# Buffers of 4 and 8 KB per partition for a fused attention and mixture-of-experts layer on one core

## The chip, the core and the metric

The kernel runs on one core of a Trainium2 chip. The metric is the device time of one execution in microseconds (us). Matrix products run on PE (TensorE); DVE, ACT and POOL (VectorE, ScalarE, GpSimd) do the rest; SP (SyncE) issues most DMAs, which 16 DMA engines carry out. On-chip memory (SBUF) has 128 partitions; a buffer's size is given per partition.

## What is computed

The reference, cut to one layer (512 tokens, width 1024, float32):

```python
h = rmsnorm(x, mix_norm);  z = h @ w_in
x = x + concatenate([pool_mixer(u, ...), dsa_attention(q, k, v, qi, ki, wi)]) @ w_out
h = rmsnorm(x, xattn_norm)
x = x + memory_cross_attention(h, mem, ...)        # 256 memory tokens
h = rmsnorm(x, ffn_norm)
x = x + hierarchical_moe(h, ...)                   # top-1 of 4 groups, top-2 of its 8 experts
# each of the 32 experts: out += (silu(h @ w_gate) * (h @ w_up) * gate) @ w_down
# w_gate, w_up: 1024 x 256; w_down: 256 x 1024; so each expert matrix is 1 MB
```

The sparse attention (`dsa_attention`) keeps the 128 best keys of each query by an indexer score.

## The kernel before

**Three stages.** Until about 280 us the kernel projects, finds the best keys (`topk`), attends and adds the output projection; until about 345 us it does the cross-attention and its projections and the routing (`ffn_in`, `route`, `seats`); from about 365 us it runs the experts (`moe_pass`). Weights of the first two stages are loaded raw and split in two float32r parts, `hi` on ACT (L257) and `lo` on DVE or POOL (L259), and multiplied in three products (`mm3`, L342 to L344). Expert weights are used raw in float32.

**Buffers.** All large tiles live in `Slots` (L61): 42 slots of 4 KB (`NSLOT`), and 8 more (`NSLOT2`) once the work area of the first stages is given up (L1148), 50 in all. `get` takes the slot that has been free longest, `put` hands slots back at the end of the list. `take_out` removes a slot for good: the experts take eight in this way, three for gathered rows, two for the turned rows `xt`, two for the results `y`, one for the selection table (`buffer`, `own`). So 42 slots are left for expert weights.

**Loads.** `Stream` (L93) holds all weight loads as one list. `pump` runs whenever something is put back or needed: it splits what is loaded and issues the next load while more than `reserve` slots are free. `do_load` (L247) issues one DMA of 512 KB on SP for each item (L249). The order of the list is written out by hand; where in the program a load is issued follows from when slots come free. SP carries out its DMAs in order, and each waits until the last reader of its slot is done. An expert matrix is two items, its halves `c` = 0 and 1, each with 4 KB per partition out of 8 KB that lie together in HBM (`add_experts`, L1129 to L1139). The items of a pair come as c = 0 of both experts, then c = 1 of both.

**Experts.** Two experts at a time form a pair (`experts`, L1193; 16 pairs), 64 token places each. For pair i PE multiplies gate (32 matmuls, L1203; c = 0 to 7, at each c both experts), transposes the hidden values of pair i - 1 (L1219), turns the gathered rows of pair i + 1 (L1072), multiplies up (L1203), then down of pair i - 1 (L1230). POOL gathers rows with an indirect DMA (`fetch`, L1059) and scatters results into `out` with an accumulating one (L1235). `fetch(i + 3)` in pair i makes, for each second pair, new index tables (`slot_rows`, L1040: `idx`, six buffers); a new `idx` may be written once the scatter that read the old one has landed.

Of the kernel before, what the change touches and what calls it, by code (L numbers as in the profile page):

```python
# [16 lines left out]
P = 128  # L17
# [18 lines left out]
O_U, O_Q, O_K, O_V, O_QI, O_KI = 0, 512, 1024, 1536, 2048, 2560  # L36
NSLOT = 42
NSLOT2 = 8
NG_BUF = 3
# [21 lines left out]
class Slots:  # L61


    def __init__(self, pool, n):
        self.pools, self.free, self.n, self.where = {}, [], 0, {}
        self.on_put = lambda: None
        self.more(pool, n)

    def more(self, pool, n):
        self.pools.update({s: pool for s in range(len(self.pools), len(self.pools) + n)})  # L70
        self.free += list(self.pools)[-n:]

    def get(self, shape, dt):
        s = self.free.pop(0)
        self.n += 1
        t = self.pools[s].tile(shape, dt, tag=f"s{s}", name=f"s{s}_{self.n}")
        self.where[id(t)] = (s, t)
        return t

    def take_out(self):  # L80
        return self.free.pop(0)

    def again(self, s, shape, dt):
        self.n += 1
        return self.pools[s].tile(shape, dt, tag=f"s{s}", name=f"s{s}_{self.n}")

    def put(self, *tiles):
        for t in tiles:
            self.free.append(self.where.pop(id(t))[0])
        self.on_put()  # L90


class Stream:  # L93
# [28 lines left out]
    def pump(self, need=None):  # L122
        if self.busy:
            return
        self.busy = True
        while True:
            force = need is not None and need not in self.out
            keep = 0 if force else self.reserve
            if self.raw and len(self.S.free) >= 2 + keep or self.raw and self.items[self.n_out][4] == "raw":
                self.out_next()  # L130
            elif (self.n_load < len(self.items) and len(self.S.free) >= 1 + keep
                  and (len(self.raw) < self.raw_max)):
# [59 lines left out]
def kernel(ctx, tc, A, out, dbg=None):  # L192
# [9 lines left out]
    ps_tr = ctx.enter_context(tc.tile_pool(name="ps_tr", bufs=PRM["tr"], space=bass.MemoryType.PSUM))  # L202
    S = Slots(slot_pool, NSLOT)

# [283 lines left out]
    def evac_k(t, ps):  # L488
# [10 lines left out]
        if t % 2 == 0:  # L499
            kT[t // 2] = [S.get([P, 2, 4, P], F32R) for _ in range(2)]  # L500
        WV.defer(PRM['lat'], lambda: split_T(qr, kT[t // 2][0][:, t % 2], kT[t // 2][1][:, t % 2], ("kT", t)))
# [95 lines left out]
    def load_bands():  # L597
        pw["b"] = [S.get([P, 1024], F32R) for _ in range(2)]
# [140 lines left out]
    def memory():  # L739
# [8 lines left out]
        dve.tensor_tensor(gqk, vecs[:, V_QN:V_QN + 1], vecs[:, V_KN:V_KN + 1], op=OP.mult)  # L748
        kmT.extend(S.get([P, MH, MT], F32R) for _ in range(2))
        vm.append(S.get([P, 2, 512], F32))  # L750
# [76 lines left out]
    def transposed(t):  # L827

        hl = [S.get([P, NC, P], F32R) for _ in range(2)]
        for k in range(2):  # L830
# [298 lines left out]
    def add_experts(n):  # L1129
        order = [(i - d, name) for i in range(NPR + 1) for d, name in ((0, "gate"), (0, "up"), (1, "down"))]  # L1130
        for i, name in order:
            for c in range(2) if 0 <= i < NPR else ():
                for k, e in enumerate(pairs[i]):
                    w = A[f"w_{name}"][e]
                    if name == "down":
                        src, shape = w.rearrange("(p k) d -> p k d", k=2)[:, c], [P, D]
                    else:
                        src, shape = w.rearrange("(p k) f -> p k f", k=NC)[:, 4 * c:4 * c + 4], [P, 4, FF]
                    ST.add((n, i, name, k, c), src, shape, eng="raw")  # L1139

# [6 lines left out]
    fin = ctx.enter_context(tc.tile_pool(name="fin", bufs=2, reuse_waits="tile"))  # L1147
    S.more(ctx.enter_context(tc.tile_pool(name="slots2", bufs=1, reuse_waits="tile")), NSLOT2)  # L1148
    ST.pump()
# [43 lines left out]
    def experts(n, i, before):  # L1193
# [4 lines left out]
        for u, name in enumerate(("gate", "up")):  # L1198
            W = {(k, c): ST.take((n, i, name, k, c)) for k in range(2) for c in range(2)}
            for c in range(NC):  # L1200
                for k in range(2):
                    ks = slice(k * CAP, (k + 1) * CAP)
                    pe.matmul(pg[ks, u], xt[:, c, ks], W[k, c // 4][:, c % 4],  # L1203
                              start=(c == 0), stop=(c == NC - 1), skip_group_check=True)
            S.put(*(W[k, c] for c in range(2) for k in range(2)))
            if u == 0:
# [9 lines left out]
    def rest(n, i, hid, idx):  # L1216
# [5 lines left out]
        yield  # L1222
        W = {(k, c): ST.take((n, i, "down", k, c)) for k in range(2) for c in range(2)}
        y = own("y", i % 2, [P, D], F32)
        py = [mm_tile([P, 512]) for _ in range(2)]
        for c in range(2):
            for m in range(2):
                for k in range(2):
                    ks = slice(k * CAP, (k + 1) * CAP)
                    pe.matmul(py[m][ks], hT[:, c, ks], W[k, c][:, m * 512:(m + 1) * 512],  # L1230
                              start=(c == 0), stop=(c == 1), skip_group_check=True)
        act.copy(y[:, :512], py[0])  # L1232
        dve.tensor_copy(y[:, 512:], py[1])  # L1233
        S.put(*(W[k, c] for c in range(2) for k in range(2)))
        pool.indirect_dma_start(out=out, out_offset=bass.IndirectOffsetOnAxis(ap=idx, axis=0),  # L1235
# [122 lines left out]
```

## Time and profile before

| what | value |
|---|---|
| time, median of 3 runs (lowest, highest) | 621.26 us (620.33, 622.89) |
| time of the profiled execution | 623.07 us |
| its span | 621.2 us |
| PE, DVE, ACT, POOL busy | 558.6, 312.9, 191.7, 115.1 us |
| queue of SP: packets, bytes, share of 16 DMA engines | 47024, 134.62 MB, 59.6% |
| expert weight loads | 192 DMAs of 512 KB |

The span is from the first to the last instruction of the profiled execution; a share is of the span. The DMA share is the mean busy share of the 16 DMA engines; it can pass 1 a little, as packets overlap. The granted clock of PE stands as a share of full speed. "A <- B" in a list of waits says that A stood idle until B was done.

### The profile page before, as it was taken

What the parts mean: (1) busy time and instruction counts of PE and PEld (TensorE: products, weight loads), DVE (VectorE), ACT (ScalarE), POOL (GpSimd) and SP (SyncE); (2) the same over time, 40 slices, a digit from 0 to 9 for tenths busy, and PEclk for the clock granted to TensorE, in tenths of its full rate; (3) what the DMA queues carried; (4) which work ended last, traced back from release to release, by engine and by line L of the source; (5) the groups of instructions that cost most, each with busy time, mean ns of one, the idle gap of its engine ahead of it and who ended that gap; (6) DMA issues with size and microseconds to landing.
All of it is one profiled execution on the core that took longest, in us unless ns stands there. A gap on an engine that the chain in (4) does not pass through costs nothing.

```text
span 621.2 us, 9049 instructions
## 1 busy us (share of the span) xinstructions
PE 558.6 (90%) x3408; PEld 395.8 (64%) x3408; DVE 312.9 (50%) x752; ACT 191.7 (31%) x366; POOL 115.1 (19%) x94
## 2 busy tenths in 40 slices
PE   8997989999979999999989589979898979899880
PEld 4776766887767777788878466555555555555430
DVE  4598999998996656544435723222222222022000
ACT  5573534424555567764432110101010100001000
POOL 0323331201363000030001211121212121211111
PEclk9998999999989999999989759979897989899996
DMA  8963021326661201129999849999999999999962
GB/s 291 379 207 103 1 69 68 121 82 190 217 216 41 79 0 35 32 79 324 336 338 365 309 135 344 396 397 391 399 382 386 357 383 360 390 355 372 339 222 32
DMA packets 52833, 147.86 MB, mean 238 GB/s; under 512 B 10288, under 2 KB 11056, under 8 KB 52784
## 3 DMA queue, kind: packets, MB, share of 16 engines
q1 hardware_dynamic: 47024, 134.62, 59.6%
q0 software_dynamic: 4608, 8.40, 5.6%
q10 hardware_dynamic: 1152, 4.19, 1.7%
q8 instruction: 29, 0.48, 0.3%
q14 instruction: 20, 0.16, 0.1%
HBM read 142.99 MB, written 12.58 MB: 250 GB/s over the span
## 4 chain that ended last, share of the span: by engine, by line
PE 65%; DMA 15%; DVE 9%; issue 4%; ACT 3%; POOL 2%; SPq 0%; POOLq 0%; DVEq 0%; ACTq 0%
PE mm L1203 15%; PE mm L342 9%; PE mm L343 9%; PE mm L344 8%; PE mm L1230 8%; DMA out_dram<-s,idx 6%; DMA s<-in_w_up_dram 2%; PE sc L352 2%; PE sc L1072 2%; DMA s<-in_w_down_dram 2%; DMA s<-in_w_in_dram 2%; PE tr L1034 2%; PE tr L919 1%; PE tr L698 1%; PE tr L711 1%
## 5 line engine op out<-in xcount | busy, mean ns | idle before, releaser
L1203 PE MATMUL mm<-s,s 128*64 128x256 f32 x1024 | 135.9, 409 | 5.5 <-ACT sg L1208 3.5
L342 PE MATMUL mm<-s,s 128*128 128x512 f32 (+1 forms) x320 | 132.5, 417 | 0.9 <-ACT s L257 0.7
L343 PE MATMUL mm<-s,s 128*128 128x512 f32 (+1 forms) x320 | 127.6, 399 | 1.2 <-DVE s L259 0.8
L344 PE MATMUL mm<-s,s 128*128 128x512 f32 (+1 forms) x320 | 127.6, 399 | 0.0
L1203 PEld LDWEIGHTS mm<-s,s 128*64 128x64 f32 x1024 | 80.1, 147 | 54.7 <-issue 15.3
L342 PEld LDWEIGHTS mm<-s,s 128*128 128x128 f32 (+1 forms) x320 | 60.6, 190 | 16.7 <-issue 2.8
L343 PEld LDWEIGHTS mm<-s,s 128*128 128x128 f32 (+1 forms) x320 | 60.7, 190 | 14.8 <-DVE s L259 1.7
L344 PEld LDWEIGHTS mm<-s,s 128*128 128x128 f32 (+1 forms) x320 | 60.7, 190 | 13.9 <-issue 0.9
L1230 PE MATMUL mm<-s,hT 128*64 128x512 f32 x256 | 64.7, 604 | 1.2 <-issue 1.2
L1232 ACT COPY s<-mm 128x512 f32<-128x512 f32 x16 | 9.4, 585 | 153.1 <-PE mm L1230 153.1
L259 POOL TENSOR_TENSOR s<-s,s 128x1024 fp32r<-128x1024 f32 x17 | 41.2, 2428 | 74.0 <-ACT s L257 72.7
L1235 POOL DMA_INDIRECT out_dram<-s,idx x16 | 25.4, 1584 | 147.0 <-DVE hT L1221 49.4
L257 ACT CAST s<-s 128x1024 fp32r<-128x1024 f32 (+1 forms) x42 | 42.2, 1018 | 30.2 <-DMA s<-in_xattn_wkv_dram 9.4
L1213 DVE SCALAR_TENSOR_TENSOR sg<-mm,gc,sg 128x256 f32<-128x256 f32 x16 | 7.7, 484 | 66.6 <-PE mm L1203 66.6
L1230 PEld LDWEIGHTS mm<-s,hT 128*64 128x64 f32 x256 | 22.0, 141 | 29.1 <-issue 23.5
L259 DVE TENSOR_TENSOR s<-s,s 128x1024 fp32r<-128x1024 f32 (+1 forms) x25 | 33.2, 1331 | 7.0 <-ACT s L257 5.7
L1233 DVE COPY s<-mm 128x512 f32<-128x512 f32 x16 | 11.1, 692 | 48.3 <-PE mm L1230 48.3
L1208 ACT ACTIVATE sg<-mm,gc 128x256 f32<-128x256 f32 x16 | 7.6, 474 | 77.7 <-PE tr L1219 40.3
L1059 POOL DMA_INDIRECT s<-hd,idx x16 | 16.6, 1038 | 72.9 <-DVE idx L1040 66.4
L587 DVE MAX8 m<-s 128x8 f32<-128x256 f32 (+2 forms) x48 | 26.6, 554 | 0.3
L1073 DVE TENSOR_TENSOR s<-sc,gcol 128x1024 f32<-128x1024 f32 x16 | 19.6, 1222 | 13.1 <-PE sc L1072 13.1
L588 DVE MATCH_REPLACE8 s<-m,s 128x256 f32<-128x256 f32 (+2 forms) x48 | 26.0, 541 | 0.0
(209 smaller groups left out, 697.7 us busy)
## 6 DMA issues: line engine op xcount, KB each, us to landing
s<-in_w_up_dram SPq DMA_DIRECT2D x64, 512.0 KB, 11.4
s<-in_w_gate_dram SPq DMA_DIRECT2D x64, 512.0 KB, 11.6
s<-in_w_down_dram SPq DMA_DIRECT2D x64, 512.0 KB, 11.4
s<-in_w_in_dram SPq DMA_DIRECT2D x20, 512.0 KB, 7.4
s<-in_x_dram SPq DMA_DIRECT2D x8, 512.0 KB, 7.8
s<-in_xattn_wkv_dram SPq DMA_DIRECT2D x8, 512.0 KB, 4.8
s<-in_w_out_dram SPq DMA_DIRECT2D x8, 512.0 KB, 4.3
s<-in_xattn_wq_dram SPq DMA_DIRECT2D x4, 512.0 KB, 4.2
```

The lines of the kernel that those rows point to most:

```text
L257: act.copy(hi, raw)
L259: eng.tensor_tensor(lo[:, c], raw[:, c], f32(hi[:, c]), op=OP.subtract)
L342: pe.matmul(ps, ah, bh, start=start, stop=False)
L343: pe.matmul(ps, ah, bl, start=False, stop=False)
L344: pe.matmul(ps, al, bh, start=False, stop=stop)
L587: dve.max(m8, a)
L588: dve.match_replace(a, m8, a, TAKEN)
L1059: pool.indirect_dma_start(out=buffer("g", i % NG_BUF, [P, D]), out_offset=None, in_=hd, in_offset=bass.IndirectOffsetOnAxis(ap=tabs_[i][0] ...
L1073: dve.tensor_tensor(xt, pt, gcol[:, :, None].to_broadcast([P, NC, P]), op=OP.mult)
L1203: pe.matmul(pg[ks, u], xt[:, c, ks], W[k, c // 4][:, c % 4], start=(c == 0), stop=(c == NC - 1), skip_group_check=True)
L1230: pe.matmul(py[m][ks], hT[:, c, ks], W[k, c][:, m * 512:(m + 1) * 512], start=(c == 0), stop=(c == 1), skip_group_check=True)
L1235: pool.indirect_dma_start(out=out, out_offset=bass.IndirectOffsetOnAxis(ap=idx, axis=0), in_=y, in_offset=None, bounds_check=T - 1, oob_is ...
```

## The change

The slots become 18 buffers of 4 KB and 12 of 8 KB, with 4 more of 8 KB in place of the eight late slots; 42 and 50 units of 4 KB as before. The eight buffers taken out for good are of 4 KB. The `hi` and `lo` of a weight tile (and other pairs that live equally long) are the two halves of an 8 KB buffer if one is free, else two of 4 KB. A single tile takes a 4 KB buffer, and when there is none, half of an 8 KB buffer, whose other half may then hold another single tile of the same type. An 8 KB buffer is free again when both halves are put back. An expert matrix is now one item of 8 KB per partition, loaded by one DMA of 1 MB into an 8 KB buffer if one is free (and was freed no later than the two oldest 4 KB ones), else as two DMAs of 512 KB into two 4 KB buffers. Both experts' matrices are handed back after the last matmul that reads them. The reserves, the lists and the order of the products stay. The core of the diff:

```diff
-NSLOT = 42
-NSLOT2 = 8
+N_ONE, N_TWO, N_TWO_MORE, N_OWN = 18, 12, 4, 8
...
     def get(self, shape, dt):
+        if self.free1:
+            s = self.free1.pop(0)
+            return self.hold(self.tile(s, shape, dt), s, None)
...
+        at = next((p for p in self.spare if p[2] == dt), None)
+        if at is None:
+            s = self.free2.pop(0)
+            t = self.tile(s, [P, 2, 1024], dt)
+            self.left[s] = 1
+            half = 0
+            self.spare.append((s, t, dt))
+        else:
+            self.spare.remove(at)
+            s, t, _ = at
+            self.left[s] += 1
+            half = 1
...
+    def get_pair(self, shape, dt):
+        if not self.free2:
+            return [self.get(shape, dt) for _ in range(2)]
+        s = self.free2.pop(0)
+        t = self.tile(s, [P, 2, *shape[1:]], dt)
+        self.left[s] = 2
+        return [self.hold(t[:, i], s, t) for i in range(2)]
+
+    def get_whole(self, shape):
+        two, ones = self.free2[:1], self.free1[:2] if len(self.free1) >= 2 + self.owed else []
+        when = lambda v: max(self.freed[s] for s in v)
+        half = [shape[0], shape[1] // 2, *shape[2:]]
+        if two and (len(ones) < 2 or when(two) <= when(ones)):
+            s = self.free2.pop(0)
+            t = self.tile(s, shape, F32)
+            self.left[s] = 2
+            h = shape[1] // 2
+            return [(slice(None), t)], [self.hold(t[:, i * h:(i + 1) * h], s, t) for i in range(2)]
+        h = shape[1] // 2
+        parts = [self.get(half, F32) for _ in range(2)]
+        return [(slice(i * h, (i + 1) * h), p) for i, p in enumerate(parts)], parts
+
+    def room(self, shape, keep):
+        if int(np.prod(shape[1:])) <= 1024:
+            return len(self.free) >= 1 + keep
+        return len(self.free) >= 2 + keep and (bool(self.free2) or len(self.free1) >= 2 + self.owed)
...
     def put(self, *tiles):
+        self.clock += 1
         for t in tiles:
-            self.free.append(self.where.pop(id(t))[0])
+            s, of, _ = self.where.pop(id(t))
+            if of is None:
+                self.free1.append(s)
+            else:
+                self.left[s] -= 1
+                if self.left[s]:
+                    continue
+                self.spare = [p for p in self.spare if p[0] != s]
+                self.free2.append(s)
+            self.freed[s] = self.clock
         self.on_put()
...
     def do_load(src, shape):
+        if int(np.prod(shape[1:])) > 1024:
+            loads, parts = S.get_whole(shape)
+            for c, t in loads:
+                sp.dma_start(t, src[:, c])
+            return parts
...
-        hi, lo = S.get(shape, F32R), S.get(shape, F32R)
+        hi, lo = S.get_pair(shape, F32R)
...
-            for c in range(2) if 0 <= i < NPR else ():
-                for k, e in enumerate(pairs[i]):
...
+            for k, e in enumerate(pairs[i] if 0 <= i < NPR else ()):
+                m = {"down": 2, "gate": NC, "up": NC}[name]
+                ST.add((n, i, name, k), A[f"w_{name}"][e].rearrange("(p k) f -> p k f", k=m), [P, m, 2048 // m], eng="raw")
...
-            W = {(k, c): ST.take((n, i, name, k, c)) for k in range(2) for c in range(2)}
+            W, held = expert(n, i, name)
...
-            S.put(*(W[k, c] for c in range(2) for k in range(2)))
+            S.put(*held)
```

`expert` takes both whole matrices of a pair and returns them with a function that finds the slice of expert k and step c. The other calls of `get_pair` are for `kT`, `kmT`, the band matrices and the transposed `x`.

## Rows read from the trace of the kernel before

**Rows 1.** The page: the profiled execution.

```profile
span 621.2 us, 9049 instructions
```

**Rows 2.** Windows: stretch, length, busy PE, PEld, DVE, ACT, POOL, PEclk, DMA share, GB/s.

```profile
33.00:42.00 9.00, 9.00 (x44) 7.44 (x43) 8.96 (x11) 7.77 (x12) 2.40 (x1) 1.00 0.99 348
...
360.00:380.00 20.00, 19.04 (x127) 13.36 (x128) 4.82 (x11) 0.47 (x1) 1.99 (x2) 0.73 0.59 190
380.00:420.00 40.00, 36.53 (x260) 22.77 (x261) 11.37 (x27) 2.59 (x5) 7.25 (x6) 0.91 1.02 389
...
500.00:590.00 90.00, 81.30 (x569) 46.46 (x567) 18.45 (x36) 6.35 (x12) 13.63 (x10) 0.96 1.01 366
380.00:590.00 210.00, 192.98 (x1359) 113.86 (x1358) 48.65 (x101) 15.30 (x29) 34.60 (x26) 0.94 1.02 377
```

**Rows 3.** Waits of SP's DMA queue, 380 to 600 us: total us, times, longest.

```profile
SPq L249 <- DMA s<-in_w_gate_dram: 51.6, 44, 3.8
...
SPq L249 <- PE mm L1203: 9.4, 19, 3.5
```

**Rows 4.** Waits of PE from 365 us on: total us, times, longest.

```profile
PE tr L1034 <- DVE idx L1040: 11.7, 4, 3.5
...
PE mm L1203 <- DMA s<-in_w_up_dram: 1.4, 1, 1.4
```

**Rows 5.** Chain that ended last, 395 to 418 us: start, us, what.

```profile
403.64 9.05 DMA out_dram<-s,idx
...
413.03 1.01 PE tr L1034 x4
```

**Rows 6.** Timeline, last pairs, PE: start, us, what [idle before <- releaser].

```profile
558.16 1.04 PE L1072 MATMUL sc<-cst,s 128*128 128x128 f32 x8
...
572.63 3.63 PE L1203 MATMUL mm<-s,s 128*64 128x256 f32 x32
...
576.86 3.67 PE L1203 MATMUL mm<-s,s 128*64 128x256 f32 x32 [0.59 <-ACT sg L1208]
...
584.37 2.48 PE L1203 MATMUL mm<-s,s 128*64 128x256 f32 x18
...
593.75 1.73 PE L1203 MATMUL mm<-s,s 128*64 128x256 f32 x13 [1.42 <-DMA s<-in_w_up_dram]
...
598.51 2.25 PE L1230 MATMUL mm<-s,hT 128*64 128x512 f32 x8
```

**Rows 7.** Chain that ended last, its last pieces.

```profile
602.24 5.77 DMA out_dram<-s,idx
```

**Rows 8.** The page, a DMA queue: packets, MB, share of 16 engines.

```profile
q8 instruction: 29, 0.48, 0.3%
```

**Rows 9.** Timeline, start of the experts, SP's issues.

```profile
368.75 0.81 SPq L249 DMA_DIRECT2D s<-in_w_down_dram  x2
371.61 3.77 SPq L249 DMA_DIRECT2D s<-in_w_gate_dram  x4
```

**Rows 10.** The same timeline, PE.

```profile
365.05 6.53 PE L1203 MATMUL mm<-s,s 128*64 128x256 f32 x32
```

**Rows 11.** Scatters into out (the tile `out_dram`): who waited; landing times.

```profile
  DVE idx L1040: 24.3, 5
...
DMA to landing us min/median/max: 5.8/8.9/10.0
```

**Rows 12.** Chain that ended last, 340 to 366 us: the first gather.

```profile
354.18 6.74 DMA s<-hd,idx
```

**Rows 13.** Waits of SP's DMA queue over the whole span.

```profile
SPq L249 <- PE mm L344: 113.3, 18, 25.6
```

**Rows 14.** Chain that ended last, first stage.

```profile
138.29 6.64 DMA s<-in_xattn_wkv_dram
```

**Rows 15.** Waits of PE, 120 to 280 us.

```profile
PE mm L343 <- DVE s L259: 0.5, 1, 0.5
```

**Rows 16.** The page, a group of instructions: busy us, mean ns | idle before.

```profile
L342 PE MATMUL mm<-s,s 128*128 128x512 f32 (+1 forms) x320 | 132.5, 417 | 0.9 <-ACT s L257 0.7
```

More of the change, by code (lines that the diff above doesn't have):

```diff
@@ L61, with __init__ @@
 class Slots:
-    def __init__(self, pool, n):
-        self.pools, self.free, self.n, self.where = {}, [], 0, {}
-        self.on_put = lambda: None
[L67 to L71, printed above, removed]
-    def get(self, shape, dt):
[L74 to L78, printed above, removed]
+    def __init__(self, pool, ones, twos):
+        self.pool_of, self.free1, self.free2, self.spare = {}, [], [], []
+        self.where, self.left, self.n, self.clock = {}, {}, 0, 0
+        self.freed = {}
+        self.owed = N_OWN
+        self.on_put = lambda: None
+        self.more(pool, ones, twos)
@@ new lines, in more, with free, tile @@
+    def more(self, pool, ones, twos):
+        for k, (free, n) in enumerate(((self.free1, ones), (self.free2, twos))):
+            for _ in range(n):
+                s = len(self.pool_of)
+                self.pool_of[s] = pool
+                self.freed[s] = 0
+                free.append(s)
+    @property
+    def free(self):
+        return range(len(self.free1) + 2 * len(self.free2) + len(self.spare))
+    def tile(self, s, shape, dt):
+        self.n += 1
+        return self.pool_of[s].tile(shape, dt, tag=f"s{s}", name=f"s{s}_{self.n}")
@@ L80, in take_out @@
+    def room(self, shape, keep):
+        if int(np.prod(shape[1:])) <= 1024:
+            return len(self.free) >= 1 + keep
+        return len(self.free) >= 2 + keep and (bool(self.free2) or len(self.free1) >= 2 + self.owed)
     def take_out(self):
[L81 to L85, printed above, removed]
+        self.owed = max(0, self.owed - 1)
+        return self.free1.pop(0)
@@ L87, in put @@
+    again = tile
     def put(self, *tiles):
+        self.clock += 1
         for t in tiles:
-            self.free.append(self.where.pop(id(t))[0])
+            s, of, _ = self.where.pop(id(t))
[8 more added lines that the diff above has]
+            self.freed[s] = self.clock
@@ L130, in pump @@
                 self.out_next()
-            elif (self.n_load < len(self.items) and len(self.S.free) >= 1 + keep
+            elif (self.n_load < len(self.items) and self.S.room(self.items[self.n_load][2], keep)
                   and (len(self.raw) < self.raw_max)):
@@ L499, in evac_k @@
         if t % 2 == 0:
-            kT[t // 2] = [S.get([P, 2, 4, P], F32R) for _ in range(2)]
+            kT[t // 2] = S.get_pair([P, 2, 4, P], F32R)
         WV.defer(PRM['lat'], lambda: split_T(qr, kT[t // 2][0][:, t % 2], kT[t // 2][1][:, t % 2], ("kT", t)))
@@ L597, in load_bands @@
     def load_bands():
-        pw["b"] = [S.get([P, 1024], F32R) for _ in range(2)]
+        pw["b"] = S.get_pair([P, 1024], F32R)
         pw["w"] = S.get([P, 4, P], F32)
@@ L748, in memory @@
         dve.tensor_tensor(gqk, vecs[:, V_QN:V_QN + 1], vecs[:, V_KN:V_KN + 1], op=OP.mult)
-        kmT.extend(S.get([P, MH, MT], F32R) for _ in range(2))
+        kmT.extend(S.get_pair([P, MH, MT], F32R))
         vm.append(S.get([P, 2, 512], F32))
@@ L827, in transposed @@
     def transposed(t):
-        hl = [S.get([P, NC, P], F32R) for _ in range(2)]
+        hl = S.get_pair([P, NC, P], F32R)
         for k in range(2):
@@ L1131, in add_experts, with expert @@
         for i, name in order:
-            for c in range(2) if 0 <= i < NPR else ():
-                for k, e in enumerate(pairs[i]):
[L1134 to L1139, printed above, removed]
+            for k, e in enumerate(pairs[i] if 0 <= i < NPR else ()):
+                m = {"down": 2, "gate": NC, "up": NC}[name]
+                ST.add((n, i, name, k), A[f"w_{name}"][e].rearrange("(p k) f -> p k f", k=m), [P, m, 2048 // m], eng="raw")
+    def expert(n, i, name):
+        W = [ST.take((n, i, name, k)) for k in range(2)]
+        m = {"down": 1, "gate": 4, "up": 4}[name]
+        return lambda k, c: W[k][c // m][:, c % m], [t for w in W for t in w]
     add_experts(0)
@@ L1147 @@
     fin = ctx.enter_context(tc.tile_pool(name="fin", bufs=2, reuse_waits="tile"))
-    S.more(ctx.enter_context(tc.tile_pool(name="slots2", bufs=1, reuse_waits="tile")), NSLOT2)
+    S.more(ctx.enter_context(tc.tile_pool(name="slots2", bufs=1, reuse_waits="tile")), 0, N_TWO_MORE)
     ST.pump()
@@ L1222, in rest @@
         yield
-        W = {(k, c): ST.take((n, i, "down", k, c)) for k in range(2) for c in range(2)}
+        W, held = expert(n, i, "down")
         y = own("y", i % 2, [P, D], F32)
@@ L1233, in rest @@
         dve.tensor_copy(y[:, 512:], py[1])
-        S.put(*(W[k, c] for c in range(2) for k in range(2)))
+        S.put(*held)
         pool.indirect_dma_start(out=out, out_offset=bass.IndirectOffsetOnAxis(ap=idx, axis=0),
```

15 lines of the change are left out of this document (12 added, 3 removed).

## The prediction

> **What bounds the kernel now.** I read the windows first, then the two lists of waits, then the chain and the timeline at the end of the span. The windows show three things [rows 2]. From 380 to 590 us, where the experts run, the DMA engines are never free: share 1.02 at 377 GB/s. PE is busy there for 193 of 210 us as well, so two resources are near their limits at once. Between 360 and 380 us the share is only 0.59: all buffers are full and the stream waits for the first expert.
>
> Which of the two sets the end? SP's waits speak for the DMA side: 51.6 us in 44 waits for earlier gate loads, and much the same for up and down, against 9.4 us for PE to free a buffer [rows 3]. So the stream runs at the rate of the DMA engines. PE waits for an expert's weights only at the very end: 1.4 us before up of the last pair [rows 4]. It starts with 21 matrices in store and uses that store up. From gate of pair 14 to gate of pair 15 it needs 11.7 us (572.63 to 584.37); the last pair takes 16.4 us to the end of down of pair 14 (584.37 to 598.51 + 2.25), though it turns no further rows, which cost 1.0 us [rows 6]. PE's slack against the stream is thus 16.4 - (11.7 - 1.0) = 5.7 us. That is the most that a faster stream can give back here: beyond it PE is the bound. Before that, PE's own delay is the scatter: four times the chain goes through a scatter that must land before a new index table may be written (9.05 us from 403.64, PE goes on at 413.03) [rows 5], and PE idles 11.7 us for it [rows 4]. What follows the last down, its two scatters (the first lands 5.77 us after 602.24) [rows 7], is the same before and after.
>
> **The sum, the stream's side.** (1) Longer rows. In 33 to 42 us only rows of 2 KB are loaded (`add_w`: two times 512 floats): 348 GB/s at share 0.99, so 352 at a full share, 22.0 per engine, 93 ns for a row. Rows of 4 KB: 377 / 1.02 = 370, 23.1 per engine, 177 ns [rows 2]. Two rows of 2 KB take 186 ns, one of 4 KB 177, so a row costs 9 ns beside its bytes, and one of 8 KB should take 345 ns in place of 354: 2.5% less. The upper end takes the best stretch, 389 / 1.02 = 381: 172 ns, 14 ns a row, 4.1%. The lower end is nothing: the only packets over 4 KB in the trace, the instruction queue's (0.48 MB in 29), run at 0.48 MB / (0.003 x 621.2 x 16 us) = 16 GB/s per engine, no better than the rest [rows 1, 8]. I take 2.5%, as the weight rows are nearest. When the stream starts again at 368.75 us, 21 of 96 matrices are loaded. Of the buffers left for weights 16 are of 8 KB and ten of 4 KB, so 16 of 21 matrices load whole; 57 of the 75 to come. A matrix of 1.05 MB takes 2.78 us at 377 GB/s: 57 x 2.78 x 2.5% = 4.0 us saved (0 to 6.5).
>
> The Trainium skill, "DMA: Bandwidth & Descriptors", section Bandwidth, speaks for less: it puts the loss of short descriptors down to about 3 cycles for each packet, with 32 bytes moved a cycle. By that, 8 KB would take 259 cycles in place of 262, 1.1%, and the saving would be an estimated 1.8 us; the 9 ns of the rows above are more, and the sum goes by them.
>
> (2) Later release. Now the first halves (c = 0) of gate 0 are free after 16 of 32 matmuls, and SP issues at 368.75; a whole matrix is read until the 32nd, 365.05 + 6.53 = 371.6 us [rows 9, 10]. While the engines have nothing else to do (share 0.59), the stream starts 2.9 us later: +2.9 (0, if the freed buffers happen to be 4 KB ones, to 2.9). (3) Later start at the end. Now PE runs 18 matmuls of the last up before the last half lands and about 14 after it (1.73 us); whole matrices let it start when the second has landed, with 3.67 us to go: +1.9 (0 to 1.9) [rows 6]. Together -4.0 + 2.9 + 1.9 = **+0.8 us** (-6.5 to +4.8).
>
> **The sum, PE's side.** (4) Gathers and scatters share the engines with the weights. Each has 128 rows, eight per engine. If each row waits behind one weight row, that wait grows from 177 to 345 ns, on 76% of the rows: 8 x 168 ns x 0.76 = 1.0 us for a gather or scatter. It is paid where PE waits: four scatters [rows 4] and the first gather, which takes 6.74 us and after which the experts begin [rows 12]: +5.0 us. The lower end is 0. The upper end: a scatter lands after 5.8 us at best (the queue is then almost empty) and 8.9 us in the median [rows 11], so the other traffic costs it 3.1 us; if that doubled, 5 x 3.1 = 15.5 us. I take 5.0: it comes from row times, the other blames the whole spread on weight rows. Less the slack, 5.0 - 5.7 = **-0.7 us** (-5.7 to +9.8). Other gathers have a whole pair's time and cost nothing unless they outlast it.
>
> (5) The first stages. The counts of units, reserves and lists stay, pairs and single tiles fit 12 and 18 buffers about as they come, and PE lost only 0.5 us there to a late weight split [rows 15]: I take 0 (bounds below, under the rivals). Fewer DMAs on SP (73 whole and 46 halves for 192) cost nothing either way, since SP spends its time in waits [rows 3].
>
> The end follows the later side: +0.8 us. The profiled execution took 623.07 us (span 621.2, 1.9 around it), 1.8 over the median; so 623.9 by its own time, and 621.26 + 0.8 = **622.1 us** by the median.
>
> **The rivals.**
> A, slower: the scatters pay the full price. Place: the wait for `idx`, four times, and the first gather. Price 3.1 us each: 15.5 - 5.7 = +9.8, 631.1 us. It decides (over 0.5%) from (5.7 + 3.1) / 5 = 1.8 us each. For it: PE has little else to wait for. Against: a weight row is not all that a scatter waits for. The Trainium skill, "DMA: Bandwidth & Descriptors", section Queues, rings and completion order, says that an engine alternates between queues packet by packet and empties a whole packet of several descriptors first; by that rule larger rows do lengthen the turn of the weights. The 3.1 us agree with some such wait; its size no row here shows. Chance 0.11.
> B, slower: buffers run short in the first stages. A half of an 8 KB buffer stays blocked while its other half lives, and `get_pair` takes the 8 KB buffer freed last, so a split may wait for PE where it had an old slot. SP already waits 113.3 us for PE in 18 waits (6.3 each) [rows 13], and the wkv load of 138.29 lies on the chain [rows 14]. One tile's products (12 matmuls of 0.4 us [rows 16]) later, once or twice: +4.8 to 9.6, 626 to 631 us. Against: the 0.5 us of [rows 15]. Chance 0.11.
> C, the change does not do what it says: whole buffers are rarely free, or 8 KB rows move like two of 4 KB. Then (1) is gone and (2), (3) stay: +4.8, 626.1 us. Chance 0.06.
> D, faster: rows that lie together also end what slows the later stretch, 366 against 389 GB/s [rows 2]. 90 us x 6% = 5.4 us more: 0.8 - 5.4 = -4.6, 616.7 us, within PE's slack if gathers stay as they are. For it: the rate falls while nothing but the place of the weights changes. Against: nothing shows that half rows cause it. Chance 0.28.
>
> **How the numbers follow.** The forecast keeps 0.44; its own range goes from 619.6 (saving at its upper end, 6.5 us, with (2) and (3) as taken: -1.7) to 626.1 (no saving: +4.8). A measurement of this kernel can tell about 0.5%, 3.1 us: 618.2 to 624.4. Faster: D but for 0.01, 0.27. Slower: A, B, C and the 0.04 of the forecast that lies over 624.4: 0.32. The same: the rest, 0.41. The range reaches down a little past D (615.5), and up through C and the lower half of B (629), which leaves out A and the rest of B.
>
> **What would show it.** A DMA share near 1 with 380 to 390 GB/s from 380 us; the first issue after the pause near 371.6; a median landing of scatters near 9.9 us; idle time of PE before L1034 near 16 us; no wait, or a short one, for the last up. Wrong would be: rates unchanged (C); scatters at 12 us (A); PE waiting for splits before 280 us, or the experts beginning later than 365 by over 3 us (B); over 395 GB/s with PE never waiting (D).

## The result, and the profile after

The changed kernel takes **640.55 us** (median of 4 runs, 635.72 to 644.12) where the kernel before takes 620.8 beside it: ratio 1.0316, 95% interval 1.0235 to 1.0397. That is 3% slower, outside the range of the prediction (615.5 to 629.0 us). The profiled execution took 641.47 us, its span is 639.6 (before: 621.2 [rows 1]).

The windows of the changed kernel (stretch, length, busy PE, PEld, DVE, ACT, POOL, PEclk, DMA share, GB/s), against [rows 2]:

```profile
360.00:380.00 20.00, 14.46 (x80) 11.80 (x82) 10.11 (x49) 2.28 (x4) 4.25 (x4) 0.58 0.54 178
...
500.00:590.00 90.00, 79.91 (x514) 44.83 (x511) 17.34 (x34) 5.30 (x10) 12.11 (x9) 0.96 1.02 392
380.00:590.00 210.00, 189.45 (x1304) 111.55 (x1305) 47.64 (x98) 13.21 (x25) 31.50 (x24) 0.95 1.01 394
580.00:600.00 20.00, 18.87 (x133) 10.56 (x131) 2.64 (x4) 1.53 (x3) 3.13 (x2) 1.00 0.83 301
```

From 360 to 380 us PE is busy for 14.46 us (before 19.04): the experts begin later. The stream did become faster: 394 GB/s from 380 to 590 us where it was 377, and 392 in the late stretch where it was 366. It did not help. From 580 to 600 us the DMA share is 0.83 and PE is busy for 18.87 of 20 us at full clock (before 0.95 and 17.41): at the end it is now PE that sets the time. The lists of waits say the same. First SP's DMA queue, 380 to 600 us, against [rows 3]; then PE from 373 us on, against [rows 4] (total us, times, longest):

```profile
SPq L326 <- DMA s<-in_w_gate_dram: 41.0, 20, 3.6
SPq L326 <- PE mm L1284: 30.1, 10, 5.9
```

```profile
PE tr L1114 <- DVE idx L1120: 16.0, 5, 4.5
```

SP waits 30.1 us for PE's gate and up products to free a buffer (before 9.4), and PE's list has no row for expert weights any more. Its wait for the index tables has grown from 11.7 to 16.0 us. The scatters into `out` (who waited, landing) are slower by about as much as predicted, against [rows 11]:

```profile
  DVE idx L1120: 32.8, 6
...
DMA to landing us min/median/max: 4.7/9.6/10.2
```

So where are 18 us? Three marks on PE's timeline split the span: the first gate product of pair 0, the first gate product of pair 9, the end of the last down product. Before they stand at 365.1, 495.4 and 605.8 us, after at 373.7, 504.2 and 623.7. The first stages lose 8.6 us, pairs 0 to 8 nothing (130.3 and 130.5), pairs 9 to 15 lose 9.1 (110.4 and 119.5). Second profiles of both kernels (e5, e11 below) confirm the first loss and one of about this size behind it, but not how it falls on the pairs.

**The first stages.** The weights of the output projection (`w_out`) come later. Their eight loads in the kernel before and after (duration min/median/max in ns, first and last start), then ACT, which splits them, 150 to 240 us, and DVE, 345 to 356 us, of the changed kernel:

```profile
L249 SPq DMA_DIRECT2D s<-in_w_out_dram x8: 367/368/461, 160.2 to 182.0; - x8
...
  ACT s L257: 4.2, 2
```

```profile
L329 SPq DMA_DIRECT2D s<-in_w_out_dram x8: 367/368/1247, 166.1 to 192.7; - x8
```

```profile
ACT s L337 <- DMA s<-in_w_out_dram: 15.8, 7, 4.0
```

```profile
DVE s L1107 <- DMA out_dram<-s: 2.5, 1, 2.5
```

The last load is issued at 192.7 instead of 182.0 us, because SP waits for a buffer, and ACT stands 15.8 us for them, seven times, where it was 4.2. Which buffer SP waits for shows in its own list, 100 to 240 us, of the kernel before and of the changed one:

```profile
SPq L249 <- DVE s L259: 5.1, 2, 2.7
```

```profile
SPq L329 <- DVE s L339: 32.2, 9, 10.6
```

It is one that a split is still reading (DVE's part here; for POOL's part the wait grows from 5.3 to 24.6 us). By the new `get`, a single tile takes a 4 KB buffer whenever one is free, however lately it came free, even if an 8 KB buffer has been free for long. From there a chain leads to PE: ACT waits 3.7 us for a `w_out` load until 197.6 us, DVE waits 2.9 us for ACT's next split (L343), the softmax stands behind that on DVE and ACT, and PE waits for its result `p`. The waits of PE from 176 to 240 us (changed kernel), and the windows from 200 to 220 us before and after:

```profile
PE tr L778 <- DVE p L770: 4.1, 2, 2.6
```

```profile
200.00:220.00 20.00, 20.00 (x133) 15.71 (x131) 14.41 (x48) 11.87 (x31) 1.37 (x5) 1.00 0.20 61
```

```profile
200.00:220.00 20.00, 17.42 (x99) 13.64 (x97) 13.64 (x40) 10.89 (x27) 2.24 (x6) 0.83 0.24 61
```

PE is busy for 15.8 to 17.6 us of this stretch in all seven profiles with 18 small buffers, and for 19.99 or 20.00 in the seven others. The last `mm3` product ends at 343.9 us before and 350.3 after, so 6.4 of the 8.6 us stand before the routing ends. The wait of DVE for `out_dram` above is a second shortage: the selection table falls on a buffer that held an `x` tile, and that tile is still being written out. SP's first load after the pause moves with all this:

```profile
377.21 2.05 SPq L326 DMA_DIRECT2D s<-in_w_gate_dram  x2
```

It was 368.75 [rows 9].

**The late pairs.** One late pair on PE's timeline, of the kernel before and of the changed kernel (start, us, what; down is L1230 and L1311, gate is L1203 and L1284):

```profile
568.63 1.94 PE L1230 MATMUL mm<-s,hT 128*64 128x512 f32 x8
570.50 0.44 PE L1219 MATMUL tr<-cst,sg 128*128 128x128 f32 x2
570.87 1.94 PE L1230 MATMUL mm<-s,hT 128*64 128x512 f32 x8
```

```profile
586.37 1.88 PE L1311 MATMUL mm<-s,hT 128*64 128x512 f32 x4
588.18 0.44 PE L1300 MATMUL tr<-cst,sg 128*128 128x128 f32 x2
588.55 2.36 PE L1311 MATMUL mm<-s,hT 128*64 128x512 f32 x9
590.37 0.59 PE L1284 MATMUL mm<-s,s 128*64 128x256 f32 x2
590.75 1.02 PE L1311 MATMUL mm<-s,hT 128*64 128x512 f32 x2
591.18 0.65 PE L1284 MATMUL mm<-s,s 128*64 128x256 f32 x2
591.61 0.59 PE L1311 MATMUL mm<-s,hT 128*64 128x512 f32 x1
```

Eight matmuls took 1.94 us, now four take 1.88 (each product of the text is two matmul instructions in the trace). Each expert of a pair uses its own 64 columns of the array (128*64). Before, products of the two experts stood side by side in PE's stream and overlapped; now the first expert's stand alone, then the transposes, then the second expert's. The order of PE's instructions is fixed when the program is built, and the text of the products is the same. What changed ahead of it is the list of loads: first halves of both experts, then second halves, became one whole matrix, then the other (e1 below tries that alone). The change was described as leaving the lists and the order of the products; the list of the expert loads is another one, and with it PE's order. The group of all down products (busy us, mean ns | idle before), of the kernel before and of the changed one:

```profile
L1230 PE MATMUL mm<-s,hT 128*64 128x512 f32 x256 | 64.7, 604 | 1.2 <-issue 1.2
```

```profile
L1311 PE MATMUL mm<-s,hT 128*64 128x512 f32 x256 | 73.7, 602 | 1.2 <-issue 1.2
```

The Trainium skill, "TensorEngine Tiling (Array Packing)", section Tiling Modes, says that different tiles of the array can run matmuls in parallel. The rows agree, with a condition: here the two tiles' matmuls overlapped only where they stood next to each other in PE's stream.

### The profile page after: what moved, and what is told of

Same layout as the page of the kernel before. It is cut to its first block, busy times and chain, and to the rows that moved or that the text cites. A ratio compares the mean times of both kernels' runs of the same rounds, so it can differ in the third digit from the quotient of the medians.

```text
span 639.6 us, 8901 instructions
## 1 busy us (share of the span) xinstructions
PE 568.7 (89%) x3408; PEld 400.4 (63%) x3408; DVE 316.0 (49%) x752; ACT 192.3 (30%) x366; POOL 118.4 (19%) x94
## 5 line engine op out<-in xcount | busy, mean ns | idle before, releaser
L1284 PE MATMUL mm<-s,s 128*64 128x256 f32 x1024 | 136.9, 399 | 3.4 <-ACT sg L1289 3.4
L1284 PEld LDWEIGHTS mm<-s,s 128*64 128x64 f32 x1024 | 80.5, 143 | 49.5 <-issue 11.4
L1311 PE MATMUL mm<-s,hT 128*64 128x512 f32 x256 | 73.7, 602 | 1.2 <-issue 1.2
L337 ACT CAST s<-s 128x1024 fp32r<-128x1024 f32 (+1 forms) x42 | 42.4, 1021 | 50.4 <-DMA s<-in_w_out_dram 15.8
L1311 PEld LDWEIGHTS mm<-s,hT 128*64 128x64 f32 x256 | 23.2, 138 | 36.5 <-issue 31.5
L339 DVE TENSOR_TENSOR s<-s,s 128x1024 fp32r<-128x1024 f32 (+1 forms) x25 | 31.0, 1244 | 5.4 <-ACT s L337 5.3
L1114 PE MATMUL tr<-inf,s 128*128 128x4 f32 x64 | 11.8, 296 | 18.9 <-DVE idx L1120 14.9
## 6 DMA issues: line engine op xcount, KB each, us to landing
s<-in_w_up_dram SPq DMA_DIRECT2D x26, 1024.0 KB, 16.5
```

What stands on the lines that cost most here:

```text
L1114: pe.matmul(pi[:, :n], sel[:, t, cols(i)], cols_of(t), start=(t == 0), stop=(t == NT - 1))
L1284: pe.matmul(pg[ks, u], xt[:, c, ks], W(k, c), start=(c == 0), stop=(c == NC - 1), skip_group_check=True)
L1311: pe.matmul(py[m][ks], hT[:, c, ks], W(k, c)[:, m * 512:(m + 1) * 512], start=(c == 0), stop=(c == 1), skip_group_check=True)
```

## The experiments

After these readings I had three theories. **P**: the new order of PE's down products costs about 10 us in pairs 9 to 14. **B**: the first stages lack 4 KB buffers, which costs 8.6 us before the experts. **D**: rows of 8 KB hold up scatters and gathers (rival A). The marks of all profiles stand here together; all are read or subtracted from PE's timeline of one execution each, the ratio is to runs of the kernel before beside it, "idx" is PE's wait for index tables, "weights" its wait for expert weights, "down" the busy time of the down products, all in us:

| kernel | time, ratio to before (95%) | first gate | to gate 9 | gate 9 to end | idx | weights | down |
|---|---|---|---|---|---|---|---|
| before | 620.8 | 365.1 | 130.3 | 110.4 | 11.7 | 2.0 | 64.7 |
| before, again (e5) | 622.74, one run | 363.6 | 125.0 | 116.9 | 11.9 | 5.4 | 66.0 |
| after | 640.55, 1.0316 (1.0235 to 1.0397) | 373.7 | 130.5 | 119.5 | 16.0 | 0 | 73.7 |
| after, again (e11) | 641.79, one run | 371.7 | 131.4 | 121.1 | 16.2 | 0 | 73.7 |
| e1 before, by expert | 621.2, 1.0019 (0.9985 to 1.0053) | 358.4 | 130.2 | 115.0 | 11.5 | 0 | 74.3 |
| e2 down bound together | 639.28, 1.0322 (1.0252 to 1.0392) | 370.4 | 128.2 | 121.2 | 16.9 | 0 | 61.6 |
| e3 42 small, 0 large | 620.77, 1.0035 (0.9997 to 1.0073) | 359.1 | 128.1 | 115.0 | 11.2 | 0 | 72.1 |
| e4 table first | 636.06, 1.0275 (1.0202 to 1.0348) | 363.9 | 132.9 | 119.9 | 16.5 | 0 | 73.6 |
| e6 4 KB rows | 634.54, 1.0213 (1.0138 to 1.0288) | 370.8 | 128.6 | 117.5 | 13.4 | 0 | 73.8 |
| e7 halves | 632.82, 1.0209 (1.0141 to 1.0278) | 369.5 | 128.5 | 116.0 | 12.2 | 4.7 | 66.0 |
| e8 26 small, 8 large | 626.55, 1.0106 (1.0062 to 1.0149) | 359.5 | 132.5 | 118.1 | 14.8 | 0 | 73.5 |
| e9 halves, table first | 634.95, 1.0254 (1.0202 to 1.0305) | 367.4 | 127.1 | 121.1 | 12.6 | 6.5 | 66.0 |
| e10 halves, 42 small | 620.97, 1.0008 (0.9978 to 1.0039) | 364.1 | 125.0 | 115.6 | 11.5 | 4.8 | 65.3 |
| e12 mixed list | 619.77, 0.9997 (0.9974 to 1.0021) | 362.3 | 127.8 | 112.9 | 11.6 | 3.2 | 66.1 |

**e1, the order alone, in the kernel before.**

```diff
-            for c in range(2) if 0 <= i < NPR else ():
-                for k, e in enumerate(pairs[i]):
+            for k, e in enumerate(pairs[i]) if 0 <= i < NPR else ():
+                for c in range(2):
```

> The kernel before with one edit: the half loads of a pair are listed expert by expert in place of half by half (the same 4 KB buffers, the same loads of 4 KB rows, the same bytes). Theory P (the order of PE's down products, fixed when the program is built, is what costs at pairs 9 to 14): the products of the pair's second expert now stand behind other work of PE in pairs 8 to 14, as in the changed kernel, so these pairs lose what the changed kernel lost, 1.6 to 1.7 us each and about 10 us in all: 629 to 632 us, with the first gate product still at 365.1. Theory D (the 8 KB rows or the transfers beside the scatters cost it): rows, buffers and bytes are as before, so 619 to 623. Theory B (only the first stages cost): 619 to 623 as well.

The time did not move: 1.0019. Yet the list did to the order what P says: the second expert's products stand behind the transposes, though rows, buffers and bytes are those of before. Its late pair, and its group of down products:

```profile
579.54 1.88 PE L1230 MATMUL mm<-s,hT 128*64 128x512 f32 x4
581.36 0.44 PE L1219 MATMUL tr<-cst,sg 128*128 128x128 f32 x2
581.72 2.36 PE L1230 MATMUL mm<-s,hT 128*64 128x512 f32 x9
```

```profile
L1230 PE MATMUL mm<-s,hT 128*64 128x512 f32 x256 | 74.3, 603 | 1.2 <-issue 1.2
```

Down costs PE 9.6 us more (74.3 - 64.7), but PE no longer waits for weights: the stretch from gate 9 to the end takes 115.0 us, between the 110.4 and 116.9 of the two profiles of the kernel before. There PE comes to the last pairs early and waits for the stream; here it is late and does not wait. From the first gate product to the end it needs 245.2 us, 3.3 to 4.5 more than in the two profiles of the kernel before; 9.6 less the 5.7 us of slack that the prediction read there is 3.9. The time does not show it, as the first gate product of this profile stands 5 to 7 us earlier (more on that under e10). P as I had put it, 10 us of the loss, falls.

**e2, the order taken back in the changed kernel.**

```diff
-        for c in range(2):
-            for m in range(2):
-                for k in range(2):
+        with tc.manual_schedule(engines={mybir.EngineType.PE}):
+            for c in range(2):
+                for m in range(2):
+                    for k in (1, 0):
```

> The changed kernel with one edit: the 8 down products of a pair are bound to stand together on PE, the second expert's ahead of the first's in each half. Buffers, loads and first stages are untouched. Theory P: pairs 9 to 14 win back about 10 us while the first gate product stays near 373.7: 629 to 632 us; the group of down products falls from 73.7 us busy to about 65. Theory D: the scatters and rows are as they were: 638 to 643. Theory B: 638 to 643 too.

No gain: 1.0322. The products overlap again, 16 in 3.65 us and 61.6 us in all:

```profile
586.15 0.44 PE L1300 MATMUL tr<-cst,sg 128*128 128x128 f32 x2 [0.66 <-DVE sg L1294]
586.52 3.65 PE L1312 MATMUL mm<-s,hT 128*64 128x512 f32 x16
```

```profile
PE tr L1114 <- DVE idx L1120: 9.9, 3, 4.9
PE tr L1300 <- DVE sg L1294: 5.6, 7, 1.6
```

The second fence is PE's waits from 470 us on. All 16 products now stand behind the transposes, so PE waits for the hidden values (5.6 us, seven times) where it had products of the first expert to do. Pairs 13 and 14 take 12.4 us each (13.3 in the changed kernel, 11.7 before), but pairs 9 to 11 take 64.7 instead of 58.5. Binding the products takes one cost away and makes another; it does not restore the order of before, in which half the products stand ahead of the transposes.

**e3, the first stages with small buffers only.**

```diff
-N_ONE, N_TWO, N_TWO_MORE, N_OWN = 18, 12, 4, 8
+N_ONE, N_TWO, N_TWO_MORE, N_OWN = 42, 0, 4, 8
```

> The changed kernel with 42 buffers of 4 KB and none of 8 KB up to the experts; the later ones (4 more of 8 KB, and those taken out for the experts' own use) as they are. Theory B for the first stages (a short list of 4 KB buffers, used again just after they come free, holds up the last load of w_out and the first gather): the first gate product goes back from 373.7 to about 365 to 366. The order of the down products stays as in the changed kernel for most of the late pairs, so by theory P the late loss of about 10 us stays: 630 to 634 us. If the whole loss comes from the first stages: 621 to 624. If nothing of it: 638 to 643.

This alone gives back the loss: 620.77 us, next to the case in which all of it comes from the first stages. The first gate product stands at 359.1, 14.6 earlier than in the changed kernel and 4.5 to 6 earlier than in the kernel before. But the edit also takes most of the whole loads away (20 of 96 matrices instead of 75), so it does not tell the buffers of the first stages from the 8 KB rows. That is what e6 to e8 and e10 are for.

**e4, the selection table takes its buffer first.**

```diff
+    owned["sel", 0] = S.take_out()
     owned.update({(name, n): S.take_out() for name in ("xt", "y") for n in range(2)})
```

> The changed kernel with one edit: the selection table takes its buffer ahead of the two gather buffers, not behind them. Theory B2 (the table falls on a buffer whose rows are still being written out, 2.5 us of wait on VectorE at 352.8 and 3.2 us on PE): the first gate product comes 2 to 3 us earlier, 371 to 372, and the end with it, 637 to 639 us. If other work ends last there (the x tile's own write, the routing): no change at 365 to 374 us and 640 at the end.

636.06 us; DVE's wait for the `x` tile is gone, the first gate product stands at 363.9, 8 to 10 us earlier than in the two profiles of the changed kernel. That is more than expected at this mark, but 2 to 4 us of it stand already at the last `mm3` product (346.0 against 348.3 and 350.3), ahead of the table. By the ratios (1.0275 for 1.0316) the time won is 2.5 us, within the noise, and in e9 the same edit won nothing.

**e6, rows of 4 KB in the whole buffers.**

```diff
-            return [(slice(None), t)], [self.hold(t[:, i * h:(i + 1) * h], s, t) for i in range(2)]
+            return ([(slice(i * h, (i + 1) * h), t[:, i * h:(i + 1) * h]) for i in range(2)],
+                    [self.hold(t[:, i * h:(i + 1) * h], s, t) for i in range(2)])
```

> The changed kernel with one edit: each whole matrix goes into its 8 KB buffer by two transfers with rows of 4 KB in place of one with rows of 8 KB. Buffers, their order of use and the order of PE's products stay. Theory D (8 KB rows hold up the scatters and gathers): PE's waits for the index table fall from 16.0 to about 12 us and the time to 634 to 638. Theories P and B (order of the products, first stages): rows of 4 KB lower the stream to 377 to 389 GB/s, but PE sets the end, so 638 to 643. If the long rows were a gain that the rest hides: 643 to 647.

634.54 us, ratio 1.0213 where it was 1.0316: as D has it, and below what P and B had. The intervals overlap, so the gain in time (about 6 us) is not clear of noise, but the waits go the same way. The edit changes two things at once, the length of the rows and the number of loads. Window, PE's wait, and scatters (who waited, landing) of this kernel:

```profile
380.00:590.00 210.00, 192.62 (x1322) 112.81 (x1320) 47.62 (x99) 14.24 (x27) 33.04 (x25) 0.94 1.01 374
```

```profile
PE tr L1115 <- DVE idx L1121: 13.4, 4, 4.1
```

```profile
  DVE idx L1121: 25.0, 5
...
DMA to landing us min/median/max: 6.2/9.1/10.2
```

The whole loads with long rows are what makes the stream faster (394 against 374 GB/s) and also what makes the scatters land later and the tables wait. By number of whole loads with 8 KB rows, the wait for tables is 11.2 to 13.4 us in all kernels with 0 or 20 of them, 14.8 with 56 (e8), 16.0 to 16.9 with 75 (after, e2, e4, e11). The median landing of the scatters is 8.9 to 9.1 us in the first group and 9.6 to 9.9 in the other two.

A wait of PE also costs more than its length. Two rows of the timeline and two windows of the changed kernel:

```profile
482.57 0.94 PE L1114 MATMUL tr<-inf,s 128*128 128x4 f32 x4 [3.19 <-DVE idx L1120]
483.44 4.95 PE L1284 MATMUL mm<-s,s 128*64 128x256 f32 x21
```

```profile
484.00:488.00 4.00, 4.00 (x22) 2.25 (x20) 1.05 (x4) 0.00 (x0) 0.00 (x0) 0.50 0.97 383
...
492.00:496.00 4.00, 4.00 (x35) 2.41 (x31) 0.69 (x1) 0.47 (x1) 1.62 (x1) 1.00 1.01 422
```

Behind 3.19 us of idling the granted clock is 0.50 (1.2 GHz) though PE is busy all the time, and 1.00 (2.4 GHz) some microseconds later. 21 matmuls of up took 4.95 us; 32 take 3.67 in the late pairs [rows 6]. But this is so in every kernel here: from 380 to 590 us the mean granted clock is 0.95 in the changed kernel, 0.94 in e6 and 0.94 before [rows 2], so the clock does not set them apart.

**e7, the changed buffers, but the experts by halves in the order of before.** Its core (the places that read `W` as in the kernel before; half loads leave the 4 KB buffers that are owed alone):

```diff
-            for k, e in enumerate(pairs[i] if 0 <= i < NPR else ()):
...
+            for c in range(2) if 0 <= i < NPR else ():
+                for k, e in enumerate(pairs[i]):
```

> The changed kernel with its 8 KB and 4 KB buffers, but the experts' matrices loaded by halves in the order of the kernel before (half by half, 4 KB rows). The first stages are those of the changed kernel; the down products of the late pairs stand as in the kernel before (both experts' halves together). Theory P + B: the first gate product stays at 370 to 374, pairs 9 to 15 win back 4 to 9 us: 631 to 636. Theory B alone (all of the loss is the first stages): 638 to 642. Theory D (the whole loads themselves cost it): back to 620 to 624.

632.82 us, where P and B together had it: no whole loads, no new order (down 66.0), and still 2.1% slower. What is left is the first stages. PE's waits here:

```profile
PE mm L1286 <- DMA s<-in_w_up_dram: 2.4, 3, 1.1
PE mm L1286 <- DMA s<-in_w_gate_dram: 1.3, 2, 0.9
PE mm L1313 <- DMA s<-in_w_down_dram: 1.0, 1, 1.0
```

At its end the stream sets the time, as before. It starts again at 373.2 us (before 368.75) with 40 half loads issued ahead instead of 42, and its last load is issued at 602.0 (before 593.8). So the late first stage reaches the end also by way of the stream, which cannot go on until the first expert has been read. That shared 8 KB buffers come free late does not slow it further: from its restart to its last issue it takes 1.51 to 1.52 us for each half load, as it did before.

**e8, 26 small and 8 large buffers.** The same line as in e3, with 26, 8, 4, 8.

> The changed kernel with 26 buffers of 4 KB and 8 of 8 KB up to the experts in place of 18 and 12 (the same bytes). Theory B (few buffers of 4 KB, used again just after they come free): part of the 14.6 us between the changed kernel (first gate at 373.7) and the one with 42 and none (359.1) comes back, so the first gate product at 362 to 368 and 625 to 634 us. If what counts is that tiles of one life share a buffer at all, and not how many: at 370 to 374, and 637 to 642 us.

626.55 us, within B's range. The first gate product stands at 359.5, before the range given for B and as early as with 42 small ones: for the first stages 26 and 8 are enough, 18 and 12 are not. What happens between was not tried. The loads of `w_out` in this kernel:

```profile
L329 SPq DMA_DIRECT2D s<-in_w_out_dram x8: 367/368/421, 150.0 to 178.7; - x8
its engine sat idle before it (us, times) until:
who waited for it (us, times):
```

The last is issued at 178.7 and ACT does not wait for any; SP's wait for DVE's part of a split, 100 to 240 us, is 6.4 us here (32.2 in the changed kernel). What this kernel still loses lies behind the first gate product: 250.6 us to the end, against 243.1 in e3 and 240.7 to 241.9 in the kernel before. It has 56 whole loads, a wait for tables of 14.8 us and down products of 73.5.

**e9 and e10, combinations.** e9 is e7 with the edit of e4; e10 is e7 with 42 and 0 as in e3.

> The kernel of e7 (buffers of 4 and 8 KB, the experts by halves as before) with the edit of e4 as well (the selection table takes its buffer first). If the losses add, this is e7 less what e4 won (640.6 to 636.1 us, 4.5): 627 to 629.5 us, the first gate product at 363 to 366; what is then left above the kernel before (7 to 9 us) is the late last load of w_out and the shorter list around 280 to 306 us. If in e7 the stream already set the end by itself (pairs 14 and 15 wait for weights there) and does not start earlier with the gate product: 631 to 633.

> The changed kernel's code with 42 buffers of 4 KB up to the experts (e3) and the experts by halves as in the kernel before (e7): no loss of the first stages, none of the order, no rows of 8 KB; 4 buffers of 8 KB remain behind the first stages. If the three losses are all there is: the first gate product at 358 to 361 as in e3, the last pairs waiting for the stream, 614 to 620 us, equal to the kernel before or up to 0.8% faster. If the first stages gain only with the list of loads expert by expert: 618 to 622 with the first gate product at 363 to 366.

e10 equals the kernel before (1.0008), with the first gate product at 364.1: the changed buffer code costs nothing by itself. This is the second case of its expectation. The profiles with the list expert by expert and buffers enough (e1, e3, e8) have the first gate product at 358.4 to 359.5, those with the list by halves (before, e5, e10) at 363.6 to 365.1. With one profile each and no cause found this is an observation, and e12 comes out between; but it means that e1 and e3 reach the time of the kernel before with an earlier start and a slower rest.

e9 won nothing (634.95, above both its ranges): DVE still waits there 2.3 us for an `x` tile, so the table came to another buffer that was not free, and PE waits 6.5 us for weights at the end. What e4 won, if anything, hangs on which buffer the table happens to meet.

**e5 and e11, the same kernels again.** 

> The kernel before, unchanged, for a second profile. In the first profile the first gate product starts at 365.1, in the kernel that only lists the half loads expert by expert at 358.4, though nothing of its first stages was changed; one step of VectorE (L981) took 1.77 us there in place of 0.16. If 365.1 was that execution's own, this profile has the first gate product at 357 to 361; if the list of loads sets it, at 364 to 366. From gate of pair 9 to the end of the last down 110 us, as in the first profile (89.0 to gate of pair 15, 21.4 behind it).

> The changed kernel, unchanged, for a second profile. The first has the first gate product at 373.7, the kernels with the same first stages (e2, e6, e7) at 369.5 to 370.8. If 373.7 was that execution's own, this profile has it at 369 to 372 and the end at 635 to 640 us; else at 373 to 375 and 640 to 643.

They show how far a single profile carries. The kernel before has its first gate product at 363.6, just before the second range, and reaches gate 9 6.8 us earlier than in the first profile, and still ends at the same time (605.5 and 605.8), since the stream ends there; from gate 9 on it takes 116.9 us and not 110. The changed kernel has 371.7, as in the first case, and ends at 624.2, with a time as in the second. The loss of the first stages in the profiles is 6.6 to 10.1 us by these pairs, the loss behind them 8.1 to 11.8. By the second profiles more of the latter lies in pairs 0 to 8 (125.0 and 131.4) than in pairs 9 to 15 (116.9 and 121.1), so where it lies is open.

**e12, an attempt to beat both.** The kernel before, with pairs 0 to 7 listed as in e1 and the others as before.

> The kernel before with one edit: the half loads are listed expert by expert for pairs 0 to 7 (as in e1) and half by half for pairs 8 to 15 (as before). e1 had its first gate product at 358.4 and the first load after the pause at 362.1 (before: 365.1 and 368.75; a second time 363.6 and 367.0), but lost 1.6 us in each late pair on PE. If the list sets both, this has the early start (358 to 360) and the late pairs of before (11.7 us for pairs 13 and 14, down products adjacent); the stream needs 223 to 226 us from its first load after the pause to its last, so the end is 4 to 6 us earlier: 613.5 to 616.5 us, 0.6 to 1.0% faster. If the early start of e1 was that execution's own: 618 to 622.

No difference (0.9997). The first gate product stands at 362.3, not at 358 to 360, and the last pairs wait for the stream. No kernel of the study is faster than the kernel before.

**The account**, by ratios times 620 us: halves instead of whole loads in the changed kernel (after to e7) 1.07%, 6.6 us; then small buffers in the first stages (e7 to e10) 2.01%, 12.5 us. The second step is clear of noise, as the intervals of e7 and e10 do not meet. The first is loose: those of after and e7 overlap, and the same step between e4 and e9 is 0.2%, 1.3 us. From e8 to e10, whose intervals do not meet, it is 0.98%, 6.1 us, but with other buffers too. Of the 6.6, whole loads with rows of 8 KB carry 6.4 (after to e6, not clear of noise either), release and order together 0.2 (e6 to e7). That last figure does not make the order free: e6 is bound by PE at its end, e7 by the stream, and they meet. Whole loads with the order of before were not had in any run, so what the faster stream would be worth on a PE that can use it stays open.

## Why the prediction was wrong

- **Step (5), "the first stages ... I take 0", failed**, and it is the largest part: 12.5 us by e7 and e10. Rival B named the place, with 4.8 to 9.6 us and a chance of 0.11. Its cause was a split that waits for a buffer; what the runs show is a load that waits for the split before it (SP 32.2 us for DVE's part, before 5.1), and then ACT and PE behind that load. What I had put against B, 0.5 us of PE's wait for late splits [rows 15], says that the old list of 42 equal buffers had room; it says nothing of a list of 18. The counts of units stayed, but a single tile goes to the short list of 4 KB buffers as long as one is free there; with 26 of them the loss of the first stages is gone (e8). B's price also left out that the stream starts later too.
- **The order of PE's products** was taken as fixed (the change leaves its text alone). A new list of loads moved it: down 64.7 to 74.3 us busy in e1, 73.7 in the changed kernel. That it moves because the second expert's weights are expected later is my reading and was not tried. In the kernel before this costs 3.3 to 4.5 us behind the first gate product and nothing measurable in the whole (e1); in the changed kernel it means that PE sets the end and no wait for weights is left to be won back.
- **Step (1)**, the faster stream: right in kind and too small. 4.0 us were taken for 2.5%, with 4.1% as the upper end; it was 394 against 377 GB/s, 4.5%. None of it reached the end. PE's side had grown by 9.0 us of down products and 4.3 us of waits for tables, 13.3 in all, against the slack of 5.7 us that (4) subtracts. An estimate from these is 7.6 us later behind the first gate product; the profiles lost 8.1 to 11.8 there.
- **Step (4)**, scatters: landing 9.6 us (predicted 9.9), wait for tables 16.0 (about 16): right in sum, with some luck in the terms. The four waits grew by 0.8 us each (11.7 to 14.9 together, 1.0 was taken), a fifth of 1.1 us came to them, and the first gather landed 4.2 us after its issue, not later than the 6.7 before. Whether the price of 5.0 us was too low is not shown: e6 puts the rows at about 6 us and is not clear of noise. What failed is the -0.7 that was left of it, since the slack was taken up by more than the scatters.
- **Steps (2), (3)**: the first issue after the pause is 3.5 us behind the first gate product (377.21 to 373.7) as it was 3.7 before (368.75 to 365.1), so (2), 2.9 us, did not appear (its lower end, 0); the 32 gate matmuls took 5.2 us there and 6.5 before, so this comparison is rough. PE never waits for the last up, so (3) had no place.
- Rival A needed scatters of 12 us: not seen. C: no, the whole loads are there (75 of 96, predicted 73). D: the rate came (392 GB/s late), the gain did not.

## What to carry to other kernels

A buffer pool split into sizes is two pools: check each against the stage that uses it most tightly, not their sum, and look at which buffer is taken next, not only at how many are free. Where the order on an engine is worked out when the program is built, a new list of loads can be a new order of compute: look at the instruction order of the changed kernel before pricing anything else. When two resources are both near their limits, a gain on one is worth only what the other leaves, and a loss on the other takes that away: here 394 GB/s came with 13.3 us more on PE. An unchanged time can hide a gain and a loss of the same size (e1).

## What the runs showed of the hardware

- Matmuls of 128x64 tiles of the two column halves overlapped in these kernels only where they were neighbours in PE's stream: 8 in 1.94 us side by side, 4 in 1.88 us alone, 16 in 3.65 us when bound together.
- A load of 1 MB with 8 KB rows in place of two of 512 KB with 4 KB rows, in the same buffers: 394 against 374 GB/s from 380 to 590 us (after, e6), and scatters of the same kernel land at 9.6 instead of 9.1 us in the median.
- Behind a wait of 3.19 us the granted clock was 0.50 from 484 to 488 us, with PE busy throughout, and 1.00 from 492 us on.
